# The order of weights and token chunks in the middle k pairs of a projection tile

## The chip, the cores and the metric

The kernel runs on one core of a Trainium2 chip. The metric is the time of one execution on the device, in microseconds (us); lower is better. The time of a kernel is the median of several runs.

The engines are called as in the profile: PE is TensorE (matmuls), PEld its weight loads, DVE is VectorE, ACT is ScalarE, POOL is GpSimd and SP is SyncE, which issues most DMAs here.

## The reference

One step of a decoder layer on 1024 prompt tokens and 8 x 4 sample tokens, 1056 in all, width 2048. One input projection feeds four groups of heads; their outputs are joined and go through one output projection:

```python
xn = rms_norm(x, norm_w)
proj = xn @ w_in
(ml_q, ml_k, ml_v, ml_o, ml_z, ml_i, ml_f, ssd_z, ssd_xbc, ssd_dt,
 sc_b, sc_c, sc_h, sc_z, rg_x, rg_z) = split_columns(proj)
...
h_ml, c1, n1, m1 = mlstm_chunkwise(q, k, v, i_pre, f_pre, c0, n0, m0, chunk)
...
y_ssd, s1 = ssd_chunkwise(xs_, dt, a_coef, bm, cm, s0, chunk)
...
cu, sc_buf1 = causal_conv(u, sc_buf, sc_conv_w)
...
r = jax.nn.sigmoid(jnp.einsum('btnd,nde->btne', xb, rg_wa) + rg_ba)
ig = jax.nn.sigmoid(jnp.einsum('btnd,nde->btne', xb, rg_wx) + rg_bx)
h_rg, h1 = rglru_scan(xr32, r, ig, rg_lambda, h0)
...
mix = jnp.concatenate([y_ml, y_ssd, y_sc, y_rg], axis=-1)
y = x + mix @ w_out
```

A final RMS norm and the new states of the four groups are returned as well. All of it is float32.

## The kernel before, in words

**Matmuls in three parts.** Input and weights are each split into a high and a low part (`xh`, `xl`, `wh`, `wl`), of type float32r. A product is `wh·xh + wh·xl + wl·xh`, so three matmuls for each block of 128 rows of k. `mm6` (L278 to L284) issues six: for the two k blocks of a weight pair, L282 (`wh`, `xh`), L283 (`wh`, `xl`) and L284 (`wl`, `xh`), all six into one PSUM bank. A matmul names its weight each time, and each has its own weight load.

**The input projection** (`in_proj`, L1277) goes over 54 tiles of 128 output columns (the first two tiles of the 56 are made in the start-up). A tile has three token chunks of 352, each with a bank of its own; four banks (0 to 3) go round in turn (`pj`), so a tile takes three and the next one starts in the fourth. k is 2048: eight weight pairs `ke` of two blocks. For each pair `w_next` gives `wh` and `wl`, and then for each of the three chunks stand six matmuls and one `tick`. So there are 18 matmuls and three ticks to a pair. At the first pair the banks are opened (`start`); at the last pair (`ke == 7`) `evac` has DVE read each bank as soon as its six matmuls are done (L586, L593).

**Weights.** SP loads a pair (L252), ACT copies it to `wh` (L264) and DVE makes `wl` (L265). There are four buffers of each; the next pairs are split while the present one is in use. ACT waits until PE has read a buffer for the last time.

**Lanes.** The four groups of heads are written as generators, in two queues (`lanes`). A `tick` lets the head of each queue issue its next piece, on any engine, up to its next `yield`; `yield n` lets n-1 ticks pass. So the ticks set where the small matmuls of the groups stand between the large ones on PE, and how much other work lies between two steps of a group. Their banks are 4, 5 and 6, in turn (`mx`), and bank 7 for the RG-LRU.

Two groups matter below. The RG-LRU gates (`rglru`, L1164) make, for each of three chunks and two halves, two matmuls into bank 7 (L1196, L1197); one tick later ACT reads the bank in two pieces (L1201, L1202); one tick after that the second half writes the same bank:

```python
                P.matmul(b[:, :CH], wh[:, cs], yy, start=True, stop=False)
                P.matmul(b[:, :CH], wl[:, cs], yy, start=False, stop=True)
                if s and c < 2:
                    halves(c + 1)
                yield 1
                S.activation(gr[pa, ts], b[pa, :CH], AF.Tanh, bias=self.rgs[pa, j:j + 1], scale=0.5)
                S.activation(gi[pa, ts], b[px, :CH], AF.Tanh, bias=self.rgs[px, 4 + j:5 + j], scale=0.5)
                yield 1 + s
```

The mLSTM (`mlstm`, L776) goes over chunks of 128 tokens, one every two ticks: three matmuls (L899, L900, L902), of which L902 reads the state of the chunk before, and then DVE makes the new state (L907). The SSD group (`ssd`, L984) has a step of one chunk every ten ticks or so (L1108, L1111, L1114 on PE, then DVE up to L1127); its convolutions are on DVE (L944).

**The output projection** (`out_proj`) uses `mm6` too: in its first part two chunks of 352 tokens, so a new bank every six matmuls; in its last part one chunk, so 48 matmuls in a row into one bank.

In the profile a matmul of type float32r shows as one record, a float32 one as two.

Of the kernel before, what the change touches and what calls it, by code (L numbers as in the profile page):

```python
# [21 lines left out]
CH = 352  # L22
# [86 lines left out]
class Build:  # L109
# [168 lines left out]
    def mm6(self, bank, wh, wl, ke, t0, n, first, last, ks=(0, 1)):  # L278
        for k in ks:
            kk = 2 * ke + k  # L280
            xh, xl = self.xh[:, kk, t0:t0 + n], self.xl[:, kk, t0:t0 + n]
            self.P.matmul(bank[:, :n], wh[:, k, :], xh, start=first and k == 0, stop=False)  # L282
            self.P.matmul(bank[:, :n], wh[:, k, :], xl, start=False, stop=False)  # L283
            self.P.matmul(bank[:, :n], wl[:, k, :], xh, start=False, stop=last and k == 1)  # L284


    def rsqrt(self, v, w, t, scale=1.0):
# [989 lines left out]
    def in_proj(self):  # L1277
        for n in range(2, len(TILES)):
            key = TILES[n]
            a = self.slot_tick()  # L1280
            if key[0] in ("B", "C", "x"):
                self.conv_in(a, 3, self.ssd_in, {"x": 0, "B": 4, "C": 6}[key[0]] + key[1])
            elif key[0] == "rx":
                self.conv_in(a, 3, self.rg_in, key[1])
            elif key[0] == "ch":
                self.conv_in(a, 2, self.sc_in, key[1])
            banks = [None] * 3
            for ke in range(8):
                wh, wl = self.w_next()
                for c in range(3):  # L1290
                    if ke == 0:
                        banks[c] = self.pj()
                    self.mm6(banks[c], wh, wl, ke, CH * c, CH, ke == 0, ke == 7)
                    if ke == 7:
                        self.evac(key, a, c, banks[c])
                        if c == 2:
                            self.done(key, a)
                    if n == len(TILES) - 2 and ke >= 4 and c == 1:
                        self.mix_load(ke - 4)
                    if n == len(TILES) - 1 and ke >= 2 and c == 1:  # L1300
                        self.mix_split(ke - 2)
                        self.mix_load(ke + 2)
                    self.tick()
# [282 lines left out]
```

## Time and profile before

| what | value |
| --- | --- |
| median of 3 runs | 1801.14 us (1799.97 to 1801.76) |
| the profiled execution | 1800.25 us |
| its span, first to last instruction | 1798.5 us |
| mean granted TensorE clock | 0.997 |
| start-up, until the first tile of `in_proj` | about 63 us |
| input projection (54 tiles), with the lanes | about 63 to 1413 us |
| output projection | about 1413 to 1784 us |
| closing norm and output | about 1784 to 1798 us |

The profile is one execution. Its rows give a group of instructions by line, engine and operation, with the tile that it writes and those that it reads, the count, the busy time in us, the mean of one in ns, and the idle time of the engine before them with what ended it. A timeline row gives start and duration in us. Matmuls overlap in the pipeline, so the duration of one is longer than the step from one start to the next; the step is what counts.

### The profile page before, as it was taken

The numbers are of one execution on the slowest core, as the hardware profiler recorded it, in microseconds if no ns is written. First come the engines' busy times: TensorE is split into PE (matmuls) and PEld (weight loads), VectorE is DVE, ScalarE is ACT, GpSimd is POOL, SyncE is SP. The second block draws the span as 40 slices with busy tenths as digits, with TensorE's granted clock in tenths as the row PEclk, the third lists the DMA queues.
The fourth block names the chain that finished last, engine by engine and source line by source line (L and its number), as shares of the span: only waits on it lengthen the run. The fifth ranks groups of instructions, "written<-read, shape, count | busy, mean of one in ns | idle before, by whom it ended". The sixth has DMA issues, their size and how long they took to land.

```text
span 1798.5 us, 30156 instructions
## 1 busy us (share of the span) xinstructions
PE 1782.8 (99%) x11459; PEld 1752.9 (97%) x11459; DVE 910.8 (51%) x2018; ACT 531.7 (30%) x1263; POOL 182.9 (10%) x244
## 2 busy tenths in 40 slices
PE   9999999999999999999999999999999999999997
PEld 8899999999999999999999999999999999999997
DVE  4493454535435444765277556544763633333664
ACT  6522122212212111331144122212441432222453
POOL 1000102011011000320000003100000011110121
PEclk9999999999999999999999999999999999999998
DMA  9411213122122122332212233321123633332774
GB/s 341 146 55 50 78 49 90 50 71 74 58 68 62 53 59 71 91 80 67 80 42 60 63 78 92 69 84 57 57 61 92 202 111 94 94 92 86 216 246 152
DMA packets 141558, 168.19 MB, mean 94 GB/s; under 512 B 18220, under 2 KB 126196, under 8 KB 140900
## 3 DMA queue, kind: packets, MB, share of 16 engines
q1 hardware_dynamic: 135492, 145.36, 28.6%
q0 software_dynamic: 5184, 19.42, 2.8%
q8 instruction: 90, 1.47, 0.3%
q10 hardware_dynamic: 736, 1.48, 0.2%
q14 instruction: 56, 0.46, 0.1%
HBM read 144.35 MB, written 21.84 MB: 92 GB/s over the span
## 4 chain that ended last, share of the span: by engine, by line
PE 91%; issue 6%; DVE 1%; DMA 0%; SPq 0%; ACT 0%; POOL 0%; DVEq 0%; ACTq 0%; POOLq 0%
PE bank L282 29%; PE bank L284 28%; PE bank L283 28%; PE bank L1114 1%; PE bank L498 0%; PE bank L900 0%; PE bank L878 0%; PE bank L899 0%; PE bank L1108 0%; DMA arena<-in_x 0%; PE bank L902 0%; PE bank L1111 0%; PE bank L876 0%; DVE arena L1443 0%; PE bank L1196 0%
## 5 line engine op out<-in xcount | busy, mean ns | idle before, releaser
L282 PE MATMUL bank<-xh,wh 128*128 128x352 f32 x3328 | 1084.6, 326 | 0.5 <-DVE arena L593 0.4
L283 PE MATMUL bank<-xl,wh 128*128 128x352 f32 x3328 | 1072.0, 322 | 1.4 <-DVE xl L474 1.4
L284 PE MATMUL bank<-xh,wl 128*128 128x352 f32 x3328 | 1071.8, 322 | 0.5 <-DVE wl L265 0.5
L282 PEld LDWEIGHTS bank<-xh,wh 128*128 128x128 f32 x3328 | 625.4, 188 | 12.9 <-issue 10.1
L283 PEld LDWEIGHTS bank<-xl,wh 128*128 128x128 f32 x3328 | 626.0, 188 | 2.2 <-DVE xl L474 2.2
L284 PEld LDWEIGHTS bank<-xh,wl 128*128 128x128 f32 x3328 | 626.2, 188 | 1.2 <-DVE wl L265 1.2
L265 DVE TENSOR_TENSOR wl<-wr,wh 128x256 fp32r<-128x256 f32 x568 | 247.9, 447 | 407.2 <-ACT wh L264 404.8
L264 ACT ACTIVATE wh<-wr 128x256 fp32r<-128x256 f32 x568 | 227.1, 413 | 593.7 <-PE bank L283 529.2
L593 DVE TENSOR_TENSOR arena<-bank,arena 128x352 f32<-128x352 f32 x114 | 58.4, 523 | 73.3 <-PE bank L284 72.8
L1359 POOL TENSOR_TENSOR arena<-arena 128x352 f32<-128x352 f32 x39 | 36.8, 948 | 316.0 <-ACT arena L1358 315.8
L944 DVE SCALAR_TENSOR_TENSOR arena<-arena 128x1080 f32<-128x1080 f32 (+1 forms) x44 | 59.9, 1362 | 1.0
L265 DVE TENSOR_TENSOR wl<-arena,wh 128x256 fp32r<-128x256 f32 x72 | 31.5, 451 | 42.3 <-ACT wh L264 42.1
L1358 ACT ACTIVATE arena<-arena 128x352 f32<-128x352 f32 x44 | 21.9, 500 | 68.4 <-DVE arena L1351 66.5
L282 PE MATMUL bank<-xh,xl 128*128 128x352 f32 x128 | 41.5, 324 | 0.0
L284 PE MATMUL bank<-xh,xl 128*128 128x352 f32 x128 | 41.4, 324 | 0.0
L264 ACT ACTIVATE wh<-arena 128x256 fp32r<-128x256 f32 x72 | 28.7, 410 | 42.6 <-PE bank L283 39.9
L283 PE MATMUL bank<-xl 128*128 128x352 f32 x128 | 41.1, 321 | 0.0
L1351 DVE TENSOR_TENSOR arena<-bank,arena 128x352 f32<-128x352 f32 x47 | 24.0, 522 | 32.7 <-PE bank L284 32.6
L586 DVE TENSOR_TENSOR arena<-bank,arena 128x352 f32<-128x352 f32 x32 | 16.4, 522 | 42.4 <-PE bank L284 42.4
L399 DVE RECIPROCAL arena<-arena 128x352 f32<-128x352 f32 (+3 forms) x18 | 35.6, 1980 | 0.2
L474 DVE SCALAR_TENSOR_TENSOR xl<-arena,xh 128x1056 fp32r<-128x1056 f32 (+1 forms) x20 | 21.7, 1095 | 23.3 <-ACT xh L471 23.3
L932 POOL COPY arena<-arena 128x3 f32<-128x3 f32 (+1 forms) x16 | 5.1, 317 | 267.1 <-DVE arena L588 267.1
(340 smaller groups left out, 1253.7 us busy)
## 6 DMA issues: line engine op xcount, KB each, us to landing
wr<-in_w_in SPq DMA_DIRECT2D x438, 128.0 KB
wr<-in_w_out SPq DMA_DIRECT2D x172, 128.0 KB
arena<-in_w_out SPq DMA_DIRECT2D x84, 128.0 KB
arena<-in_xr SPq DMA_DIRECT2D x16, 512.0 KB
arena<-rowd SPq DMA_DIRECT2D x32, 256.0 KB
mixd<-arena POOLq DMA_DIRECT2D x15, 528.0 KB, 3.8
arena<-mixd SPq DMA_DIRECT2D x15, 528.0 KB
arena<-in_x SPq DMA_DIRECT2D x14, 528.5 KB
```

What stands on the lines that cost most here:

```text
L264: self.S.activation(h, r, AF.Copy)
L265: self.V.tensor_sub(l, r, h.bitcast(F32))
L282: self.P.matmul(bank[:, :n], wh[:, k, :], xh, start=first and k == 0, stop=False)
L283: self.P.matmul(bank[:, :n], wh[:, k, :], xl, start=False, stop=False)
L284: self.P.matmul(bank[:, :n], wl[:, k, :], xh, start=False, stop=last and k == 1)
L399: self.V.reciprocal(x[:, a:b], x[:, a:b])
L474: V.scalar_tensor_tensor(self.xl[:, k, ts], x, w, self.xh[:, k, ts].bitcast(F32), op0=OP.mult, op1=OP.subtract)
L593: V.tensor_mul(a[:, t0:t0 + CH], bank[:, :CH], rs[:, t0:t0 + CH])
L944: V.scalar_tensor_tensor(y[:, :n], a[:, i:i + n], w(i), y[:, :n], op0=OP.mult, op1=OP.add)
L1351: V.tensor_add(y[:, ts], b[:, :w], y[:, ts])
L1358: S.activation(t, y[:, ts], AF.Square)
L1359: (G if nacc[gr] < KT - 1 else V).tensor_add(a[:, ts], a[:, ts], t)
```

## The change

In the six middle pairs of a tile (`0 < ke < 7`) a new function `mm18` issues the 18 matmuls of the pair: for each of the two k blocks and each of the three products, the same weight goes over the three chunks in turn. The following loop over the chunks then only ticks, three times. The first and the last pair are as before.

```diff
+    def mm18(self, banks, wh, wl, ke):
+
+        for k in (0, 1):
+            kk = 2 * ke + k
+            for w, x in ((wh, self.xh), (wh, self.xl), (wl, self.xh)):
+                for c, b in enumerate(banks):
+                    self.P.matmul(b[:, :CH], w[:, k, :], x[:, kk, CH * c:CH * c + CH], start=False, stop=False)
...
             for ke in range(8):
                 wh, wl = self.w_next()
+                mid = 0 < ke < 7
+                if mid:
+                    self.mm18(banks, wh, wl, ke)
                 for c in range(3):
                     if ke == 0:
                         banks[c] = self.pj()
-                    self.mm6(banks[c], wh, wl, ke, CH * c, CH, ke == 0, ke == 7)
+                    if not mid:
+                        self.mm6(banks[c], wh, wl, ke, CH * c, CH, ke == 0, ke == 7)
```

The line of the matmuls in `mm18` is L292. Later lines move down by 8 (from L286 to the loop in `in_proj`): the RG-LRU's L1196 and L1197 become L1204 and L1205, its L1201 and L1202 become L1209 and L1210, the mLSTM's L899, L900, L902 and L907 become L907, L908, L910 and L915, and the evacuations L586 and L593 become L594 and L601.

Only PE's order differs. The third pair of a tile on PE before, from its start (`bank0` and `bank1` are the banks of the first two chunks, `wh2` and `wl2` the pair's weight):

```order
L282 MATMUL bank0_82<-xh_65,wh2_75 128x352
L283 MATMUL bank0_82<-xl_66,wh2_75 128x352
L284 MATMUL bank0_82<-xh_65,wl2_76 128x352
L282 MATMUL bank0_82<-xh_65,wh2_75 128x352
L283 MATMUL bank0_82<-xl_66,wh2_75 128x352
L284 MATMUL bank0_82<-xh_65,wl2_76 128x352
L282 MATMUL bank1_83<-xh_65,wh2_75 128x352
L283 MATMUL bank1_83<-xl_66,wh2_75 128x352
```

The same pair on PE now:

```order
L292 MATMUL bank0_82<-xh_65,wh2_75 128x352
L292 MATMUL bank1_83<-xh_65,wh2_75 128x352
L292 MATMUL bank2_84<-xh_65,wh2_75 128x352
L292 MATMUL bank0_82<-xl_66,wh2_75 128x352
L292 MATMUL bank1_83<-xl_66,wh2_75 128x352
L292 MATMUL bank2_84<-xl_66,wh2_75 128x352
L292 MATMUL bank0_82<-xh_65,wl2_76 128x352
L292 MATMUL bank1_83<-xh_65,wl2_76 128x352
```

The bank changes at every matmul instead of at every sixth, and a weight stays for three in place of one or two.

The last token chunk of an RG-LRU tile on PE before (`bank_89` is bank 7, `fa` and `fb` hold its operands); twelve matmuls of the projection follow the first half, of which six are shown, and then come L1196 and L1197 again:

```order
L284 MATMUL bank_85<-xh,wl_76 128x352
L1196 MATMUL bank_89<-fa 128x352
L1197 MATMUL bank_89<-fa,fb 128x352
L282 MATMUL bank_82<-xh,wh_75 128x352
L283 MATMUL bank_82<-xl,wh_75 128x352
L284 MATMUL bank_82<-xh,wl_76 128x352
L282 MATMUL bank_82<-xh,wh_75 128x352
L283 MATMUL bank_82<-xl,wh_75 128x352
L284 MATMUL bank_82<-xh,wl_76 128x352
```

The same place on PE now:

```order
L292 MATMUL bank_83<-xh,wl_76 128x352
L1204 MATMUL bank_89<-fa 128x352
L1205 MATMUL bank_89<-fa,fb 128x352
L1204 MATMUL bank_89<-fa 128x352
L1205 MATMUL bank_89<-fa,fb 128x352
L282 MATMUL bank_85<-xh,wh_77 128x352
L283 MATMUL bank_85<-xl,wh_77 128x352
```

The two halves now follow each other directly. This occurs in four places, once in each RG-LRU tile.

An mLSTM step on PE before (`bank5`, `bank6` are lane banks); each step of three stands between matmuls of the projection:

```order
L284 MATMUL bank3_85<-xh_65,wl2_76 128x352
L899 MATMUL bank6_88<-arena_81 128x129
L900 MATMUL bank6_88<-arena_81 128x129
L902 MATMUL bank6_88<-arena_81 128x129
L282 MATMUL bank1_83<-xh_65,wh3_77 128x352
L283 MATMUL bank1_83<-xl_66,wh3_77 128x352
```

The same place on PE now:

```order
L292 MATMUL bank3_85<-xh_65,wl2_76 128x352
L870 MATMUL bank4_86<-arena_81 128x128 x4
L907 MATMUL bank5_87<-arena_81 128x129
L908 MATMUL bank5_87<-arena_81 128x129
L910 MATMUL bank5_87<-arena_81 128x129
L907 MATMUL bank6_88<-arena_81 128x129
L908 MATMUL bank6_88<-arena_81 128x129
L910 MATMUL bank6_88<-arena_81 128x129
L282 MATMUL bank1_83<-xh_65,wh3_77 128x352
```

Two steps of the mLSTM stand side by side. This occurs in six places.

## The prediction

> **What bounds the kernel now.** I read the page first: busy shares, granted clock, the chain that ended last, the costliest group.
>
> ```profile
> PE 1782.8 (99%) x11459; PEld 1752.9 (97%) x11459; DVE 910.8 (51%) x2018; ACT 531.7 (30%) x1263; POOL 182.9 (10%) x244
> PEclk9999999999999999999999999999999999999998
> PE 91%; issue 6%; DVE 1%; DMA 0%; SPq 0%; ACT 0%; POOL 0%; DVEq 0%; ACTq 0%; POOLq 0%
> L282 PE MATMUL bank<-xh,wh 128*128 128x352 f32 x3328 | 1084.6, 326 | 0.5 <-DVE arena L593 0.4
> ```
>
> PE is busy in 99% of the span at full granted clock, and the chain is PE's own instructions. Every matmul has its own weight load (11459 and 11459), also where two matmuls in a row use the same weight. A busy share can still hide slow matmuls, so I next asked for what PE waits for, all through the kernel.
>
> ```profile
> PE bank L283 <- DVE xl L474: 1.4, 2, 0.9
> PE bank L491 <- DVE xl L489: 1.4, 1, 1.4
> PE bank L1434 <- DVE arena L1431: 0.6, 1, 0.6
> PE bank L284 <- DVE wl L265: 0.5, 1, 0.5
> PE bank L282 <- DVE arena L593: 0.4, 1, 0.4
> PE bank L1428 <- ACT arena L1426: 0.3, 1, 0.3
> ```
>
> That is all: 4.6 us, most of it in the first and last stage. So the time is the number of matmuls times their pitch (start to start), plus the small matmuls of the lanes. Only two things can move it: the pitch, and new waits of PE. The timeline of PE around one lane insertion in the projection gives the pitch.
>
> ```profile
> 920.33 0.32 PE L1196 MATMUL bank<-fa 128*128 128x352 f32 x1
> 920.49 0.32 PE L1197 MATMUL bank<-fa,fb 128*128 128x352 f32 x1
> 920.65 0.32 PE L282 MATMUL bank<-xh,wh 128*128 128x352 f32 x1
> ...
> 921.29 0.32 PE L283 MATMUL bank<-xl,wh 128*128 128x352 f32 x1
> 921.45 0.32 PE L284 MATMUL bank<-xh,wl 128*128 128x352 f32 x1
> 921.61 0.32 PE L282 MATMUL bank<-xh,wh 128*128 128x352 f32 x1
> ...
> 922.58 0.33 PE L1196 MATMUL bank<-fa 128*128 128x352 f32 x1
> ```
>
> From 920.65 to 922.58 there are 12 matmuls, six into one bank and six into the next: 1.93 / 12 = 161 ns each. The step 921.45 to 921.61 is the change of bank: 160 ns. The step before it, within one bank, is 160 ns too.
>
> **The change, part by part.**
>
> *Counts.* 54 tiles, six pairs each, 18 matmuls each: 5832 matmuls are reordered. None is added or removed, and no weight load either. On DVE, ACT, POOL and SP the order is the same, line numbers aside, so no DMA issue, weight split or evacuation passes another. Edits with no price: the wl of a pair is first needed at its seventh matmul and not its third, and wh is last read at the fifteenth and not the seventeenth; both only lengthen waits that ACT and DVE have in hand. The first and last pair of a tile are as before, so a bank is opened and emptied as before.
>
> *Pitch.* If writing one bank again and again cost something, a stage that changes banks more often would be quicker. Two stretches of the output projection, without waits, tell: in the first the bank changes every 6 matmuls (two token chunks), in the second every 48 (one chunk).
>
> ```profile
> 1520.00:1640.00 120.00, 120.00 (x753) 120.00 (x752) 38.12 (x79) 32.51 (x79) 15.20 (x16) 1.00 0.32 91
> 1690.00:1770.00 80.00, 80.00 (x501) 80.00 (x500) 49.48 (x112) 41.01 (x105) 17.73 (x25) 1.00 0.76 238
> ```
>
> 120.00 / 753 = 159.4 ns against 80.00 / 501 = 159.7 ns: eight times as many changes are worth 0.3 ns. No stretch shows a repeated weight together with a new bank; a repeated weight (L282 to L283) steps 160 ns as the others do. So I take 0 for the pitch and keep both ends: -0.3 ns x 5832 = -1.7 us, and, from the 161 against 159.4 ns above, +1.4 ns x 5832 = +8 us.
>
> How much of the pitch could depend on a bank at all? The lane matmuls of 256 columns, of the same type, give a second point:
>
> ```profile
> 743.73 0.40 PE L1093 MATMUL bank<-fb,fa 96*128 96x256 f32 x2
> 743.97 0.33 PE L282 MATMUL bank<-xh,wh 128*128 128x352 f32 x1
> ```
>
> Two of them take 0.24 us, 120 ns each. 160 - 120 = 40 ns for 96 columns is 0.417 ns a column, 146.7 ns for 352, and 13 ns that do not grow with the columns. Only those 13 ns could go.
> The Trainium skill (TensorE: Matmul & The Clock Gate, Back-to-back issue gap) gives a warm gap of N/2.4 + 2.5 ns, which is 149.2 ns here, and names no bank in it; the trace's 160 ns does not agree. If rotating banks brought the page's gap, an estimate by it would be 10.8 ns x 5832 = 63 us less.
>
> *The three ticks now stand together.* Before, a tick of the lanes stood behind every six matmuls. Now, in the six middle pairs, 18 matmuls run first and then all three ticks follow with nothing between. Where a lane's PE work at one tick needs an ACT or DVE result that itself waits for PE work one or two ticks earlier, its cover of twelve matmuls (1.9 us) is gone if both fall into one group. Following every wait of PE back through the order, I find two such places.
>
> First, the RG-LRU gates: L1196 writes bank 7 again after ACT has read it (L1201, L1202). Two halves land side by side in four places, one for each RG-LRU tile. ACT in the same stretch:
>
> ```profile
> 920.91 0.55 ACT L1201 ACTIVATE arena<-bank,arena 64x352 f32<-64x352 f32 x1 [1.30 <-PE bank L1197]
> 921.47 0.55 ACT L1202 ACTIVATE arena<-bank,arena 64x352 f32<-64x352 f32 x1
> ```
>
> ACT ends at 921.47 + 0.55 = 922.02. Before, the next L1196 came at 922.58, after the twelve matmuls. Now it is next in PE's queue and would start at 920.65. What a release and a restart cost, from the first and last stage:
>
> ```profile
> 1786.43 0.18 DVE L1431 RECIPROCAL arena<-arena 128x3 f32<-128x3 f32 x1 [1.36 <-ACT arena L1430]
> 1786.66 0.41 PEld L1434 LDWEIGHTS bank<-arena 128*128 128x128 f32 x4 [0.64 <-DVE arena L1431]
> 13.64 0.43 PE L283 MATMUL bank<-xl,wh 128*128 128x352 f32 x1 [0.51 <-DVE xl L474]
> 13.91 0.33 PE L284 MATMUL bank<-xh,wl 128*128 128x352 f32 x1
> ```
>
> PE starts 0.05 us after the release (1786.61 to 1786.66), and the matmul after a restart comes 0.27 us later and not 0.16: 0.11 more. A wait costs 922.02 - 920.65 + 0.05 + 0.11 = 1.53 us; four cost 6.1 us. Queued behind it on PE are the next pair's matmuls, so all of it lengthens the span.
>
> Second, the mLSTM state: L902 of one chunk needs the state that DVE (L907) makes after the chunk before. Two chunks stand side by side in six places.
>
> ```profile
> 266.16 0.39 PE L900 MATMUL bank<-arena 128*128 128x129 f32 x2
> 266.38 0.39 PE L902 MATMUL bank<-arena 128*128 128x129 f32 x2
> 266.81 0.35 DVE L907 SCALAR_TENSOR_TENSOR arena<-arena,bank 128x129 f32<-128x129 f32 x1 [0.77 <-PE bank L902]
> ```
>
> One such matmul is two records, 0.22 us. After L902 at 266.38 would come L899, L900 and then L902 at 267.04. DVE is done at 267.16, with the release 267.21, and with a restart of at most 0.11: 0.17 to 0.28 us. I take 0.28; six cost 1.7 us.
>
> Every other wait of PE keeps at least 0.6 us of cover over what its chain took in the trace, or stands as before. *Sum:* 6.1 + 1.7 + 0 = 7.8 us. The profiled execution took 1800.25 us around a span of 1798.5, so it would be 1808.1; it lies 0.9 us below the median of the runs, and 1801.14 + 7.8 = 1808.9, rounded 1809.0.
>
> **The rivals.**
>
> *Rotation pays (faster).* Same-bank writes hold each matmul up by some of the 13 ns. For it: the 13 ns are there and nothing in the trace names them; repeated weight with new bank is never seen. Against it: bank changes at 160 ns, and 159.4 against 159.7. From 1.34 ns (7.8 us / 5832) it outweighs the waits; all 13 ns give 1809 - 76 = 1733 us. Less of it, 0.7 to 1.9 ns, leaves the time within 0.2% of before, about 1801 us.
>
> *Lane work piles up (slower still).* After a group of ticks, DVE has all its PE-bound work at once, and the evacuation of the tile's first bank stands behind it.
>
> ```profile
> 806.11 0.66 PE L1114 MATMUL bank<-arena 128*64 128x128 f32 x8
> 808.55 0.29 DVE L1127 TENSOR_TENSOR arena<-arena,bank 128x128 f32<-128x128 f32 x1
> L593 DVE TENSOR_TENSOR arena<-bank,arena 128x352 f32<-128x352 f32 x114 | 58.4, 523 | 73.3 <-PE bank L284 72.8
> L265 DVE TENSOR_TENSOR wl<-wr,wh 128x256 fp32r<-128x256 f32 x568 | 247.9, 447 | 407.2 <-ACT wh L264 404.8
> L944 DVE SCALAR_TENSOR_TENSOR arena<-arena 128x1080 f32<-128x1080 f32 (+1 forms) x44 | 59.9, 1362 | 1.0
> ```
>
> In an SSD step DVE ends at 808.84, 2.1 us after PE's 806.77; with one split (0.45) and one evacuation (0.52) that is 3.1 us. Until the next tile needs that bank, PE has 24 matmuls, 3.84 us. That holds, unless a convolution of the other lane (three L944, 4.1 us) stands between: 3.3 us late. If seven of some 15 convolutions meet it: 23 us, 1832 us.
>
> *The clock drops.* The windows around the end show what idle PE costs:
>
> ```profile
> 1785.00:1790.00 5.00, 1.70 (x12) 1.37 (x12) 3.03 (x9) 1.65 (x6) 1.94 (x3) 0.83 0.24 84
> 1790.00:1798.00 8.00, 0.00 (x0) 0.00 (x0) 2.54 (x6) 0.00 (x0) 1.66 (x2) 0.50 0.87 310
> ```
>
> PE idle for 3.3 of 5 us brought 0.83, and idle throughout, 0.50. If each of the four waits of 1.5 us halved the clock for 5 us, that is 4 x 2.5 = 10 us more, 1819. Against it: the stops of 1.4 us and less that PE has now do not lower the page's clock.
> The Trainium skill (TensorE: Matmul & The Clock Gate, A second HAM failure mode: psum-queue depth-cycling) tells of a kernel that cycled through PSUM banks, whose PE idled briefly between groups until the clock swung; that speaks against this change, but nothing in the trace of before shows it.
>
> *The change does not do what it says* is ruled out by the order, where banks alternate at every matmul; that weights are loaded once for three chunks it does not say, and loads stay at one for each matmul.
>
> **How the numbers follow.** About 0.2% (3.6 us) is what a measurement of this kernel can tell from no change. Forecast, waits of about 8 us at the old pitch: 0.66. Rotation pays in full or well over 1.9 ns: 0.10, faster. It pays just enough to balance the waits: 0.12, the same. Piled-up lane work 0.08 and clock 0.04, slower. Slower is 0.66 + 0.08 + 0.04 = 0.78. The forecast with its pitch ends spans 1809 - 1.7 to 1809 + 8, so 1807 to 1817. The range goes down to 1802, half of the balancing case, and up to 1820, to hold the clock case; faster and piled-up work stay outside.
>
> **What would show it.** Right: in PE's waits, L1204 (the old L1196) waiting for ACT four times, some 1.4 us each, and L910 for DVE six times, short; a step of 160 ns between the new line's matmuls, alternating banks and all. Wrong: steps under 158 ns (rotation pays) or over 161; waits of the projection's first pair for the evacuation L601; a PEclk digit below 9 in the middle.

## The result, and the profile after

The changed kernel takes 1819.6 us (median of 3 runs, 1819.5 to 1820.2) against 1801.1 before; the ratio is 1.0102, with a 95% interval of 1.0087 to 1.0117. So it is slower by 18.5 us, where 7.8 were forecast: the side is right, the forecast less than half of the measured size. The profiled execution took 1819.47 us, its span 1817.7.

The page of the kernel after: busy shares, granted clock, chain, and the groups of the new line.

```profile
PE 1795.9 (99%) x11459; PEld 1764.3 (97%) x11459; DVE 916.9 (50%) x2018; ACT 530.0 (29%) x1263; POOL 183.3 (10%) x244
PEclk9999999999999999999999999999999999999998
PE 91%; issue 6%; DVE 1%; ACT 1%; DMA 0%; SPq 0%; POOL 0%; DVEq 0%; ACTq 0%; POOLq 0%
L292 PE MATMUL bank<-xh,wh 128*128 128x352 f32 x1944 | 426.6, 327 | 0.0
L292 PE MATMUL bank<-xh,wl 128*128 128x352 f32 x1944 | 419.1, 323 | 0.0
L292 PE MATMUL bank<-xl,wh 128*128 128x352 f32 x1944 | 418.4, 323 | 0.0
```

Little is to be seen here. PE has the same instructions, the clock has the same digits (the mean granted clock is 0.997 in both), and the mean durations (322 to 327 ns) are those of before to within 1 ns. A duration that overlaps its neighbours does not show the step. PE's longest waits after:

```profile
PE bank L1204 <- ACT arena L1210: 5.1, 4, 1.3
PE bank L283 <- DVE xl L482: 1.6, 3, 0.8
PE bank L499 <- DVE xl L497: 1.4, 1, 1.4
PE bank L282 <- DVE arena L601: 1.1, 2, 0.9
```

The first line is new and is what was forecast: four waits for the RG-LRU's ACT work. The second and third belong to the start-up and were there before. The last line is the tile's evacuation, 1.1 us against 0.4 before. One of the four waits, on the timelines of PE and of ACT:

```profile
930.76 0.32 PE L1205 MATMUL bank<-fa,fb 128*128 128x352 f32 x1
932.35 0.44 PE L1204 MATMUL bank<-fa 128*128 128x352 f32 x1 [1.26 <-ACT arena L1210]
932.62 0.32 PE L1205 MATMUL bank<-fa,fb 128*128 128x352 f32 x1
```

```profile
931.74 0.55 ACT L1210 ACTIVATE arena<-bank,arena 64x352 f32<-64x352 f32 x1
```

L1204 would have come 0.16 us after 930.76, at 930.92. It comes at 932.35, 0.06 us after ACT's end at 932.29, and the next matmul 0.27 us later. That is 1.43 + 0.11 = 1.54 us, against 1.53 worked out before; four make 6.2 us. The mLSTM place, PE and DVE:

```profile
262.09 0.39 PE L910 MATMUL bank<-arena 128*128 128x129 f32 x2
262.32 0.39 PE L907 MATMUL bank<-arena 128*128 128x129 f32 x2
262.54 0.39 PE L908 MATMUL bank<-arena 128*128 128x129 f32 x2
262.92 0.49 PE L910 MATMUL bank<-arena 128*128 128x129 f32 x2
```

```profile
262.52 0.35 DVE L915 SCALAR_TENSOR_TENSOR arena<-arena,bank 128x129 f32<-128x129 f32 x1
```

At steps of 0.22 the second L910 would start at 262.76. DVE ends at 262.87, and PE goes on at 262.92: 0.16 us, and with its longer restart 0.26 in all, six times 1.6 us. Both kinds of wait together are 7.8 us, as forecast. They are not the whole of 18.5.

The rest is in the step. On PE's timeline of the kernel after, rows of three matmuls with the same weight (steps are counted from the start of the first row shown to that of a later one; `...` marks rows left out):

```profile
1060.01 0.65 PE L292 MATMUL bank<-xl,wh 128*128 128x352 f32 x3
1060.49 0.65 PE L292 MATMUL bank<-xh,wl 128*128 128x352 f32 x3
...
1062.43 0.65 PE L292 MATMUL bank<-xh,wh 128*128 128x352 f32 x3
...
1071.66 0.65 PE L292 MATMUL bank<-xl,wh 128*128 128x352 f32 x3
```

The first 15 steps, to 1062.43, take 2.42 us, 161.3 ns each; 72 steps, to 1071.66, take 11.65 us, 161.8 ns each. Before, 72 steps over the same places of the same tile:

```profile
1047.32 0.32 PE L282 MATMUL bank<-xh,wh 128*128 128x352 f32 x1
...
1058.80 0.32 PE L282 MATMUL bank<-xh,wh 128*128 128x352 f32 x1
```

11.48 us, 159.4 ns each. Over all steps of the middle pairs in the trace (start to start of two large matmuls, where no lane matmul stands between them or just before, 5,600 of them) the mean is 161.7 ns after and 159.6 before. In the first and last pair of a tile, whose order did not change, it is 159.5 in both. 2.1 ns x 5832 = 12.2 us. With the 7.8 us of waits that is 20.0 us, a little more than the 18.5 us between the medians and the 19.2 us between the two profiled spans. Part of the excess lies in the mean, which leaves out steps beside lane work: with every place of a tile counted alike the difference is 2.0 ns, or 11.7 us. The rest stays unexplained.

### The profile page after: what moved, and what is told of

The parts are those of the page before. It is cut to its first block, busy times and chain, and to the rows that moved or that the text cites. A ratio compares the mean times of both kernels' runs of the same rounds, so it can differ in the third digit from the quotient of the medians.

```text
span 1817.7 us, 30146 instructions
## 1 busy us (share of the span) xinstructions
PE 1795.9 (99%) x11459; PEld 1764.3 (97%) x11459; DVE 916.9 (50%) x2018; ACT 530.0 (29%) x1263; POOL 183.3 (10%) x244
## 4 chain that ended last, share of the span: by engine, by line
PE 91%; issue 6%; DVE 1%; ACT 1%; DMA 0%; SPq 0%; POOL 0%; DVEq 0%; ACTq 0%; POOLq 0%
PE bank L292 50%; PE bank L282 12%; PE bank L284 12%; PE bank L283 11%; PE bank L1122 1%; PE bank L910 0%; PE bank L506 0%; PE bank L908 0%; PE bank L886 0%; PE bank L907 0%; PE bank L1116 0%; DMA arena<-in_x 0%; PE bank L1119 0%; PE bank L1204 0%; PE bank L884 0%
## 5 line engine op out<-in xcount | busy, mean ns | idle before, releaser
L265 DVE TENSOR_TENSOR wl<-wr,wh 128x256 fp32r<-128x256 f32 x568 | 255.1, 461 | 397.1 <-ACT wh L264 231.6
L282 PE MATMUL bank<-xh,wh 128*128 128x352 f32 x1384 | 450.3, 325 | 1.4 <-DVE arena L601 1.1
L283 PE MATMUL bank<-xl,wh 128*128 128x352 f32 x1384 | 446.1, 322 | 1.6 <-DVE xl L482 1.6
L284 PE MATMUL bank<-xh,wl 128*128 128x352 f32 x1384 | 446.1, 322 | 0.5 <-DVE wl L265 0.5
L292 PE MATMUL bank<-xh,wh 128*128 128x352 f32 x1944 | 426.6, 327 | 0.0
L292 PE MATMUL bank<-xh,wl 128*128 128x352 f32 x1944 | 419.1, 323 | 0.0
L292 PE MATMUL bank<-xl,wh 128*128 128x352 f32 x1944 | 418.4, 323 | 0.0
L292 PEld LDWEIGHTS bank<-xh,wl 128*128 128x128 f32 x1944 | 333.5, 188 | 0.0
L292 PEld LDWEIGHTS bank<-xh,wh 128*128 128x128 f32 x1944 | 327.3, 189 | 6.0 <-issue 5.9
L292 PEld LDWEIGHTS bank<-xl,wh 128*128 128x128 f32 x1944 | 329.7, 188 | 0.0
L282 PEld LDWEIGHTS bank<-xh,wh 128*128 128x128 f32 x1384 | 260.1, 188 | 7.5 <-issue 3.5
L283 PEld LDWEIGHTS bank<-xl,wh 128*128 128x128 f32 x1384 | 260.2, 188 | 2.5 <-DVE xl L482 2.4
L284 PEld LDWEIGHTS bank<-xh,wl 128*128 128x128 f32 x1384 | 260.6, 188 | 1.3 <-DVE wl L265 1.3
L601 DVE TENSOR_TENSOR arena<-bank,arena 128x352 f32<-128x352 f32 x114 | 57.6, 523 | 66.9 <-PE bank L284 66.5
```

Source lines behind the costliest of these rows:

```text
L265: self.V.tensor_sub(l, r, h.bitcast(F32))
L292: self.P.matmul(b[:, :CH], w[:, k, :], x[:, kk, CH * c:CH * c + CH], start=False, stop=False)
L601: V.tensor_mul(a[:, t0:t0 + CH], bank[:, :CH], rs[:, t0:t0 + CH])
```

## The experiments

From here on *mean step* is that mean over the middle pairs, and *edge step* the same over the first and last pair of a tile, each from the run's own trace. Times are medians of a comparison of 3 rounds, beside runs of the kernel before on the same chip (1800.6 us for e1 to e8, e13 and e14; 1801.6 for e9 to e12).

### Order or ticks

The theory after the result (A): two costs that add up, the waits from the grouped ticks and a longer step from the order of the 18 matmuls. The rival (B): all of it comes from the grouped ticks.

**e1, ticks apart:** the new order, with a tick after every six.

```diff
-                if mid:
-                    self.mm18(banks, wh, wl, ke)
                 for c in range(3):
...
-                    if not mid:
+                    if mid:
+                        self.mm18(banks, wh, wl, ke, c)
+                    else:
                         self.mm6(banks[c], wh, wl, ke, CH * c, CH, ke == 0, ke == 7)
```

Here `mm18` takes a part and issues `todo[6 * part:6 * part + 6]` of the same list of 18.

> The new order of the 18 matmuls is kept, but a tick follows every six of them, as before the change. Theory A (the order of the 18 makes each matmul about 2 ns slower, some 11 us in all, and the grouped ticks add four RG-LRU and six mLSTM waits, some 8 us): PE's waits fall back to those of before, the step stays near 161.6 ns, about 1812 us. Theory B (all of the 18.5 us comes from the ticks that stand together, the slower step too): about 1801 us, step 159.5 ns.

**e2, ticks grouped:** the old order.

```diff
+                for c in range(3):
+                    if mid:
+                        self.mm6(banks[c], wh, wl, ke, CH * c, CH, False, False)
                 for c in range(3):
...
                     self.tick()
```

> The old order of the matmuls (six into one bank, mm6), but the three ticks of a middle pair stand together after the 18. Theory A: only the waits are left, four of about 1.5 us and six of about 0.3 us, 7.8 us: about 1809 us with a step of 159.5 ns. Theory B: about 1819 us, step over 161 ns.

Measured: e1 1812.8 us, ratio 1.0070 (1.0055 to 1.0085), mean step 161.7 ns. e2 1807.9 us, ratio 1.0042 (1.0027 to 1.0057), mean step 159.6 ns. PE's longest waits in e1, and then in e2 (the lines of e2's code lie nine lower than those of after):

```profile
PE bank L501 <- DVE xl L499: 1.4, 1, 1.4
PE bank L283 <- DVE xl L484: 1.1, 2, 0.9
```

```profile
PE bank L1195 <- ACT arena L1201: 5.1, 4, 1.3
PE bank L490 <- DVE xl L488: 1.4, 1, 1.4
PE bank L282 <- DVE arena L592: 1.3, 2, 0.9
```

B falls. The order alone costs 12.2 us and has no new wait; the ticks alone cost 7.3 us and have the four waits. 12.2 + 7.3 = 19.5 against 18.5 with both, the same within the intervals of the three.

### Bank, chunk or weight

The order changes three things at once from one matmul to the next: the bank, the token chunk that is read, and how often a weight stays. The next runs keep the ticks apart and vary `todo`, a list of (k block, weight, high or low input, chunk read, bank written):

```diff
 # e1
 todo = [(k, w, x, c, c) for k in (0, 1) for w, x in prods for c in range(3)]
 # e3
+todo = [(k, w, x, 0, c) for k in (0, 1) for w, x in prods for c in range(3)]
 # e4
+todo = [(k, w, x, c, 0) for k in (0, 1) for w, x in prods for c in range(3)]
 # e5
+todo = [(k, *prods[(s + c) % 3], c, c) for k in (0, 1) for s in range(3) for c in range(3)]
 # e6
+todo = [(k, w, x, c, c) for k in (0, 1) for w, x in prods for c in (2, 1, 0)]
```

> As with the ticks apart, but in the middle pairs all matmuls read the first token chunk, while the banks still go round (so the other two chunks' products of the middle pairs are left out). If the change of bank makes the step longer: step near 161.6 ns, about 1812 us. If the change of token chunk (where xh and xl are read) does, or the two together: step near 159.5 ns, about 1801 us. If it is the threefold repeat of a weight: 161.6 ns here too.

> As with the ticks apart, but in the middle pairs all 18 matmuls write the first chunk's bank, while the token chunks still go round (so the sums of the banks are not those of the chunks). If the change of bank makes the step longer: step near 159.5 ns, about 1801 us. If the change of token chunk does: near 161.6 ns, about 1812 us. If it is the threefold repeat of a weight: 161.6 ns here and with the banks turning alone.

Measured: e3 1802.3 us, ratio 1.0009 (1.0000 to 1.0019), mean step 159.9. e4 1813.2 us, ratio 1.0070 (1.0053 to 1.0086), mean step 161.7. 15 steps of e3 and then of e4 on PE's timeline, as shown for after:

```profile
1060.14 0.63 PE L294 MATMUL bank<-xl,wh 128*128 128x352 f32 x3
...
1062.53 0.64 PE L294 MATMUL bank<-xh,wh 128*128 128x352 f32 x3
```

```profile
1059.88 0.64 PE L294 MATMUL bank<-xl,wh 128*128 128x352 f32 x3
...
1062.30 0.65 PE L294 MATMUL bank<-xh,wh 128*128 128x352 f32 x3
```

2.39 us (159.3 ns) where the banks turn, 2.42 us (161.3 ns) where the chunks turn and all 18 go into one bank. The change of bank does not make the step longer, and neither does the weight, which stays for three matmuls in both. What counts is where `xh` and `xl` are read.

> Ticks apart; chunks and banks go round as in the change, but the three products go round with them, so that no weight is used twice in a row and xh and xl mix. If any jump between token chunks makes the step longer: 161.6 ns, 1812 us as with the ticks apart alone. If it takes a repeated weight, or chunk after chunk out of the same tile: about 159.5 ns, 1801 us.

> Ticks apart; the change's order with the chunks taken 2, 1, 0. If reading one chunk straight behind the one before it in the same tile (each start where the last ended) makes the step longer, backward starts cure it: 159.5 ns, 1801 us. If any jump between chunks does: 161.6 ns, 1812 us.

Measured: e5 1813.5 us, ratio 1.0070 (1.0055 to 1.0085); e6 1813.1 us, ratio 1.0069 (1.0054 to 1.0084); both with a mean step of 161.7. In e5 a weight stays for one matmul or for two, and not for three; it does repeat at some places (`wh` with `xh`, then `wh` with `xl`), other than the text ahead of the run says. Neither that nor chunks taken backward alter anything. The single steps show it best. For the third pair of a tile, the medians of the 18 steps in ns, over all tiles:

```
after 159 164 165 159 161 161 162 161 161 164 165 159 161 161 167 166 159 158
e4    159 164 165 159 161 161 162 162 161 164 165 158 161 161 167 167 159 158
e5    159 164 165 159 161 161 162 162 161 163 165 158 161 161 167 167 159 159
e6    159 164 165 158 161 161 162 162 162 163 165 158 161 161 167 166 159 159
before 159 161 161 160 157 161 155 160 157 161 160 160 160 160 160 161 155 160
```

Four orders with one pattern. A chunk is 352 columns of 4 bytes, 1408 bytes, which is 5.5 x 256. So, counted from the start of `xh` or `xl`, the first and the third chunk start alike within 256 bytes, and the second starts 128 bytes off, in the other half; a k block (4224 bytes, 16.5 x 256) moves all of them by 128. Taken 0, 1, 2 or 2, 1, 0, the halves alternate in the same way, and that is what e4, e5, e6 and the changed kernel share.

### Where the read starts

**e8:** the second chunk is read from column 384. **e13:** all three starts lie in the other half. **e11:** the second start is 64 bytes away from e8's.

```diff
-xs[x][:, kk, CH * c:CH * c + CH]
+xs[x][:, kk, (0, 384, 704)[c]:(0, 384, 704)[c] + CH]     # e8
+xs[x][:, kk, (32, 352, 672)[c]:(32, 352, 672)[c] + CH]   # e13
+xs[x][:, kk, (0, 368, 704)[c]:(0, 368, 704)[c] + CH]     # e11
```

> Ticks apart; the change's order, but in the middle pairs the second chunk is read from column 384 and not 352 (so its products there are those of other tokens), which makes all starts multiples of 64 columns and takes away that each chunk starts where the last ended. If the start's alignment, or the contiguous start, makes the step longer: about 159.5 ns, 1801 us. If any turn of chunks does: 161.6 ns, 1812 us.

> Ticks apart and the change's order, but in the middle pairs the chunks are read from columns 32, 352 and 672, all in the second half of 256 bytes for an even k block and in the first for an odd one (so the first and third chunk's products there are those of other tokens). If mixing halves makes the step longer: near 159.8 ns, 1802 us as with the starts moved to the first half. If a start at column 352 is slow by itself, in turn with others: 161 ns or more, 1810 us or more.

> As the run with moved starts, but the second chunk is read from column 368, 64 bytes short of a multiple of 256 (products there are those of other tokens). If halves of 256 bytes are what counts (192 lies in the second half): about 1812 us as with 352. If only a change by 128 bytes counts: about 1802 us. If any change of the start within 256 bytes counts: 1812 us or more.

Measured: e8 1802.4 us, ratio 1.0009 (0.9999 to 1.0019), mean step 159.9. e13 1801.4 us, ratio 1.0003 (0.9994 to 1.0013), 159.7. e11 1809.5 us, ratio 1.0046 (1.0029 to 1.0062), 161.0. 18 steps of e8, and 15 of e13:

```profile
1059.73 0.64 PE L294 MATMUL bank<-xh,wh 128*128 128x352 f32 x3
...
1062.60 0.64 PE L294 MATMUL bank<-xh,wh 128*128 128x352 f32 x3
```

```profile
1059.96 0.64 PE L294 MATMUL bank<-xl,wh 128*128 128x352 f32 x3
...
1062.34 0.64 PE L294 MATMUL bank<-xh,wh 128*128 128x352 f32 x3
```

2.87 / 18 = 159.4 and 2.38 / 15 = 158.7 ns. Banks and chunks turn at every matmul as in the changed kernel, and a start at column 352 is quick, once the starts within a k block lie alike. The medians of the 18 single steps of a third pair in e8 are those of e3 to within 1 ns, although e3 reads one chunk alone: what the two share is where within 256 bytes each read starts. e11 lies between the 1802 and the 1812 us that were expected, slower than e8 and quicker than e1, so a start 64 bytes off counts too, by less.

The texts ahead of the next runs speak of two theories. C: a step is longer where successive matmuls start their reads in different halves of 256 bytes. D: the turn from one chunk to another makes it longer, and the other columns read in e8 hid it.

**e10:** the converse, in the old order: only `xl` is read 32 columns off.

```diff
-            xh, xl = self.xh[:, kk, t0:t0 + n], self.xl[:, kk, t0:t0 + n]
+            xh, xl = self.xh[:, kk, t0:t0 + n], self.xl[:, kk, t0 + off:t0 + off + n]
```

`off` is 32 columns (-32 for the third chunk) in the middle pairs and 0 elsewhere.

> The order of before, ticks as before, but in the middle pairs xl is read 32 columns (128 bytes) off (so the products of xl there are those of other tokens). Bank, weight and chunk order are as before; only the start's half changes at nearly every matmul. Theory C: about 161.6 ns a step in the middle pairs, 1810 to 1814 us. Theory D: 159.5 ns, 1801 us.

Measured: 1806.8 us, ratio 1.0032 (1.0019 to 1.0045), mean step 160.6. The shift alone slows the order of before, by 1.0 ns and not by 2.1: the direction is that of theory C, the size is not, although the half changes at 16 of 18 steps here and at 14 in the changed kernel (`xh` and `xl` taken to begin alike, which e5's pattern bears out). Within 256 bytes all middle pairs have the same sequence of starts, and yet their steps follow two patterns in turn (the first of the 18 steps has a median of 159 ns in the second, fourth and sixth pair of a tile and of 156 in the third, fifth and seventh). So where two successive reads start within 256 bytes does not settle a step alone.

**e9:** starts that lie alike, and each chunk still with its own products: chunks of 320, 384 and 352 tokens in the whole input projection.

```diff
+CS = (0, 320, 704, 1056)
...
+            n = CS[c + 1] - CS[c]
-            self.P.matmul(banks[b][:, :CH], ws[w][:, k, :], xs[x][:, kk, CH * c:CH * c + CH], start=False, stop=False)
+            self.P.matmul(banks[b][:, :n], ws[w][:, k, :], xs[x][:, kk, CS[c]:CS[c] + n], start=False, stop=False)
```

`evac` and the first and last pair take the same bounds.

> Ticks apart and the change's order, but the whole input projection uses chunks of 320, 384 and 352 tokens, so that all three start at a multiple of 64 columns (256 bytes) and all products are the right ones. Theory C (a step is longer where successive matmuls start their reads of xh or xl in different halves of 256 bytes; that each chunk of 352 columns, 1408 bytes, moves the start by half makes the new order slow): mean step like the order before, about 1802 us. Theory D (it is the turn from one chunk to another, and reading other columns in the run with moved starts hid it): about 1812 us.

Measured: 1807.2 us, ratio 1.0033 (1.0022 to 1.0045), so neither of the two numbers expected. On PE's timeline, 36 steps of the middle pairs:

```profile
1290.02 0.64 PE L296 MATMUL bank<-xl,wh 128*128 128x320 f32 x3
...
1295.80 0.48 PE L296 MATMUL bank<-xl,wh 128*128 128x320 f32 x2
```

5.78 us, 160.6 ns each (a matmul of 384 columns steps about 175 ns, one of 352 161, one of 320 147). The plain mean step is 160.8 here, but it misleads: the steps that it leaves out beside lane work are those of the first and the third chunk, and in e9 the chunks differ in width. With every place of a tile counted alike, the middle pairs, in the new order, step 160.4 ns, and the edge pairs, in the old order, 160.4 too (159.5 to 159.7 in the other kernels, e12 aside); in the other kernels this way of counting changes a mean by at most 0.1. So the uneven widths cost some 0.85 ns in either order, about 6.6 us over the 7776 matmuls of all pairs, where 5.6 were measured, and the new order adds nothing, where it added 2.1 ns with the starts of 1408 bytes. The ends of the reads do not lie alike in e9 (the third chunk's lies 128 bytes off the other two within 256), so it is the start that counts here and not the end.

**e7 and e12** ask whether the cost goes with the number of changes of half.

```diff
 # e7: wh over xh and xl of each chunk, then wl over the three chunks
+todo = [(k, 0, x, c, c) for k in (0, 1) for c in range(3) for x in (0, 1)]
+todo = [t for k in (0, 1) for t in todo[6 * k:6 * k + 6] + [(k, 1, 0, c, c) for c in range(3)]]
 # e12
+turns = ((0, 2, 1), (1, 0, 2), (2, 0, 1))
+todo = [(k, w, x, c, c) for k in (0, 1) for (w, x), cs in zip(prods, turns) for c in cs]
```

> Ticks apart; wh goes over each chunk's xh and xl in turn (six in a row), then wl over the three chunks' xh. Only every second step within the six changes the chunk, and xh and xl alternate as before the change. If the length goes with the number of chunk changes (9 of 18 steps or so): about 160.5 ns, 1806 us. If alternating xh and xl is what keeps the step short: 159.5 ns for the six of wh, longer only in the three of wl, about 1804 us. If the repeat of a weight counts: over 161.6 ns, 1813 us or more.

> Ticks apart; each weight goes over the three chunks, but in an order that puts chunks with the same half together (0 2 1, 1 0 2, 2 0 1), so that of 18 steps 6 change the half, against 14 in the change's order, 10 with high and low in turn, 4 in the order of before and 2 with the moved starts. Banks and chunks still turn at most steps. Theory C, by the 0.15 ns that a change cost between 2 and 14 of 18: about 160.3 ns, 1804 to 1806 us. Theory D: about 1810 us.

Measured: e7 1808.7 us, ratio 1.0044 (1.0029 to 1.0059), mean step 161.1. e12 1811.5 us, ratio 1.0056 (1.0041 to 1.0071), mean step 161.1 and, unlike any other kernel with chunks of 352, a longer edge step, 160.4. e7 met none of its three numbers (1804, 1806 and 1813). The half changes at 10 of its 18 steps; a line through e8 (2 changes, 159.9) and e1 (14, 161.7) gives 161.1 ns for it, as measured. With 6 changes, e12 does not fit that line (1804 to 1806 expected), and it carries its delay into pairs whose order is the old one. So the count of changes is not the rule. 1811.5 is near the 1810 of theory D; but D has e9 against it, where all three chunks turn at no cost, and e14 below.

**e14:** each chunk with its own products, and the half never changes from one matmul to the next within a k block: each weight turns over the first and third chunk, and the second has its six as before.

```diff
+todo = [(k, w, x, c, c) for cs in ((0, 2), (1,)) for k in (0, 1) for w, x in prods for c in cs]
```

> Ticks apart, all products right: in a middle pair each weight goes over the first and third chunk in turn (starts at columns 0 and 704, equal half) for both k blocks, and then the second chunk takes its six as before. Two banks change at each step in twelve of 18 matmuls, and the weight repeats. If mixing halves is what counts: near 159.6 ns, 1801 to 1803 us. If the turn of chunks counts in any other way: near 161 ns, 1808 us or more.

Measured: 1801.4 us, ratio 1.0004 (0.9994 to 1.0013), mean step 159.7. On PE's timeline, rows of two matmuls into two banks:

```profile
1059.90 0.48 PE L294 MATMUL bank<-xl,wh 128*128 128x352 f32 x2
1060.21 0.48 PE L294 MATMUL bank<-xh,wl 128*128 128x352 f32 x2
1060.54 0.48 PE L294 MATMUL bank<-xh,wh 128*128 128x352 f32 x2
1060.85 0.48 PE L294 MATMUL bank<-xl,wh 128*128 128x352 f32 x2
1061.17 0.48 PE L294 MATMUL bank<-xh,wl 128*128 128x352 f32 x2
1061.49 0.32 PE L294 MATMUL bank<-xh,wh 128*128 128x352 f32 x1
```

Ten steps from 1059.90 to 1061.49, 159 ns each. So weights can go over two chunks in turn, with the banks alternating, at the price of before; nothing is gained by it. No order tried is quicker than before.

The times agree with the steps. (Mean step - 159.6) x 5832 gives 8.7 us for e7, 5.8 for e10, 8.2 for e11, 12.2 for e1 and e4, 1.7 for e3 and e8, 0.6 for e14; measured are 8.1, 5.2, 7.9, 12.2 and 12.6, 1.7 and 1.8, 0.8. For e12 the middle pairs give 8.7 and the edge pairs 1.7, 10.4 in all; measured are 9.8.

## Why the prediction was right and wrong

*Counts and orders on the other engines: right.* The counts of instructions on PE, DVE, ACT and POOL are the same after, and SP issues the same loads.

*RG-LRU and mLSTM waits: right, in place, number and size.* 6.1 and 1.7 us were forecast; the profile after has 4 x 1.54 and 6 x 0.26, and the ticks grouped without the new order (e2) cost 7.3 us. The prediction had the six short ones in the list of waits, too; they are not there, and only the timeline shows them.

*Rotation pays: rightly rejected.* Banks that turn alone (e3) leave the step at 159.9 ns, and e4, in a single bank, is as slow as the change. The 13 ns that do not grow with the columns are not the bank's.

*Pitch 0, ends -1.7 and +8 us: wrong, and this is the step that failed.* It measured +12.2 us, 2.1 ns a step, and the step of 161.7 ns is over the 161 that the prediction itself named as a sign of being wrong. The sentence that the repeated weight with a new bank is not to be seen in any row was true, but it covered two of three things. The rows compared (bank changes every 6 or every 48 matmuls) all stay on one stretch of `xh` and `xl` for the three matmuls of a k block; none moved to another stretch at every matmul. The upper end came from the spread among those rows, and so could not hold an effect that they do not have. The code of the change did show that the chunk, and with it the start of the read, changes at each matmul. That 1819.6 us lies inside the range of 1802 to 1820 is luck: its upper end was put there for the clock case, which did not come, and the forecast with its pitch ends reached only to 1817.

*Lane work piles up:* little of it. The wait for the evacuation grew from 0.4 to 1.1 us, not by 23. *The clock drops:* no. The mean granted clock is 0.997 as before, and the window from 932 to 937 us, right behind one of the four waits, shows 1.00.

What is shown: the longer step comes from where successive reads of `xh` and `xl` start (e4 against e3), and it goes when successive reads within a k block start alike within 256 bytes (e8, e13, e14, and e9 once the widths are taken off). What stays open: the rule by which a sequence of starts makes a step of 155 to 168 ns. The count of changes does not give it (e12), and in e10 the shift in the old order gave half, and pairs with one sequence of starts had two patterns of steps.
The Trainium skill (SBUF — State Buffer, Specifications (TRN2)) tells of lines of 16 bytes, with a price for each cross to a new one. Counted from the start of `xh` or `xl`, all starts here are multiples of 16 bytes, e11's too, and each matmul reads 1408 bytes in a row, so by that rule no order would differ from another; the runs differ by up to 12 us.

## What to carry to other kernels

When a loop order is turned, list everything that changes from one instruction to the next: output bank, weight, and the address of the moving operand, and look for a row of the profile for each; where there is none, the spread of the other rows is no bound. A bank that alternates bought nothing here. And where small work is placed by ticks between large matmuls, three ticks in a row are not three ticks apart: follow each wait of PE back to PE before moving them.

## What was not expected of the hardware

A float32r matmul of 352 columns steps 159.6 to 159.9 ns in the mean when the reads within a k block start alike from one to the next, whether the bank changes at every matmul or at every sixth (e3, e8, e13, e14 and before). It steps 160.6 to 161.7 ns in the mean when starts that differ by 64 or 128 bytes within 256 are mixed, by the sequence and with single steps up to 168 ns. The width matters as well: in e9 the steps are about 147, 161 and 175 ns for 320, 352 and 384 columns.
